# Bias rows as two one-pass products of stacked parts, and the gate's columns turned from a zeroed tile of 128

## The chip, the cores and the metric

The kernel runs on 1 core of one Trainium2 chip. The metric is the device time of one execution in microseconds (us). The kernel before takes 1168.48 us, the median of 3 runs (1168.42 to 1168.51).

## The reference

The kernel computes a two-layer encoder trunk for 512 tokens of width 1024, all in fp32. Layer 0 is differential attention with a shared relative-position bias; layer 1 is chunked gated linear attention (GLA). Both also attend to 256 memory tokens, and each is followed by a gated MLP with a short causal convolution. Two small pieces matter here.

```python
# layer 0: the bias that is added to the logits of each head
bias = table[t5_bucket(key_pos[None, :] - q_pos[:, None])]      # table = rel_bias, 32 x 6
logits = logits + jnp.transpose(bias, (2, 0, 1))[None, :, None]
# layer 1: the decay of each key channel, from 16 columns of the projection
log_a = jax.nn.log_sigmoid((gate_low @ gate_w + gate_b)) / GLA_GATE_TAU
```

## The kernel before, in words

**Work on TensorE.** Every large product is split: a tile is written as a high part in fp32r (a rounded fp32 that TensorE multiplies in one pass) and a low part, the remainder, and three fp32r products (high x high, high x low, low x high) add up in one PSUM bank. `split` and `split_weights` (L252 to L256, L309 to L311) make the parts: ScalarE (ACT) writes the high part, VectorE (DVE) subtracts to get the low part.

**Order.** TensorE runs in program order throughout. In the opening stage (L437 to L517, the tile pool "ini") ACT, DVE, POOL and SP run in program order too; elsewhere a scheduler orders these four. So in the opening stage an instruction that waits holds up everything written behind it on its engine.

**The opening stage.** It multiplies the normalised input with the first weight block in eight steps `k` = 0 to 7 of 12 matmuls each (L510 to L517), into four banks `first`. Ahead of step k the loop makes the operands of step k+1 (`operands`, L472 to L488). In step 4, ahead of its matmuls, `bias_rows` (L394 to L399) multiplies the bias table `rb` (32 x 6, fp32) with the one-hot matrix `oh` (32 x 640, fp32): two products on 32 rows and 6 columns of the array, each evicted by a DVE copy to 6 partitions of `bs`. In step 6 come, ahead of its matmuls: three weight blocks (`make_block`: ACT L253, DVE L256), the token sums of squares (`token_rsqrt`, L424, then L234 on DVE, L241 and L242 on ACT, and L227 to L229 on DVE), the fourth weight block, `small_vectors` (seven scalings of `cols`, then `lam`: a product and a sum on DVE, L404 and L405, an Exp on ACT, L406, and `nlam` on DVE, L407), and two writes of `bs` to DRAM (L506). Step 7 has only its matmuls. The projection of `v` (`gemm`, L330 to L332) follows at once on TensorE.

**Loads.** SP issues the loads in program order; as built, each one also waits for the one eight places ahead of it in that queue to land. Behind the loads of x and of the first weights come the first columns of the constants, `rb`, `oh`, three weight blocks of 512 KB, `cols`, the lambda vectors, the rest of the constants, the convolution columns and the fourth weight block. `bias` (L699 to L703) later reads the bias rows back from DRAM, shifted for each partition, for the first logits (L726).

**The gate in layer 1.** The projection `gm` gives 16 gate columns and 256 memory-query columns for each of four token blocks; ACT evicts them (`ev_gl`, L851 to L853), the gate columns to `gl` (128 x 4 x 16). `turn_gate` (L893 to L899) transposes the four blocks on TensorE (L896, recorded at L220), each as a product on 16 columns of the array, and makes the parts: two ACT copies (L897, L898) and a DVE subtraction (L899). The decay products (L909) wait for these.

**Tiles.** `xtile()` hands out 512-column tiles of a shared pool of 36 (tag "xs"); a tile's first writer waits until the older tile in that place is released.

Of the kernel before, what the change touches and what calls it, by code (L numbers as in the profile page):

```python
# [11 lines left out]
F32 = mybir.dt.float32  # L12
F32R = mybir.dt.float32r
# [9 lines left out]
KT = D // 128  # L23
NB = S // 128
# [155 lines left out]
def trunk(ctx, tc, head_d, x_t, mem_t, wpack, cols_a_d, cols_d, conv_d, gate_d, rel_bias, diff_lambda, consts, onehot, out):  # L180
    nc = tc.nc
    mm = nc.tensor.matmul
    V, A, G = nc.vector, nc.scalar, nc.gpsimd
# [9 lines left out]
    def bank(tag):  # L193
        return ps.tile([128, 512], F32, name=f"ps_{tag}", tag=tag)

    def xtile():
        return xs.tile([128, S], F32, name="xt", tag="xs", bufs=XS)

    def split_tiles(pool=None, tag="xs", bufs=XS):
        pool = pool or xs  # L200
        return (pool.tile([128, S], F32R, name=tag + "h", tag=tag, bufs=bufs),
                pool.tile([128, S], F32R, name=tag + "l", tag=tag, bufs=bufs))
# [4 lines left out]
    def blk(b, w=128):  # L207
        return slice(w * b, w * b + w)
# [9 lines left out]
    def transpose(dst, src):  # L218
        n = src.shape[0]
        nc.tensor.transpose(dst, src, ident[:n, :n])  # L220
# [31 lines left out]
    def split_weights(c, raw, hi, lo, pin=False):  # L252
        ins = A.copy(hi[:, c], raw[:, c])  # L253
        if pin:
            tc.keep_in_program_order(ins)
        V.tensor_sub(lo[:, c], raw[:, c], hi[:, c].bitcast(F32))  # L256

    def raw_tile():
        return wp.tile([128, WTILE], F32, name="raw", tag="raw", bufs=3)

    def load_raw(raw, n):
        nc.sync.dma_start(raw[:, :n], wpack[at[0], :, :n])
        at[0] += 1
        return raw
# [30 lines left out]
    def weights(key, by_block=False):  # L295
        i = used[0]
        assert plan[i][0] == key, (plan[i][0], key)
        limit = first_of[i] + WB if by_block else first_of[min(i + 2, len(plan))]
        while done[0] < min(max(limit, first_of[i + 1]), len(order)):
            make_block()  # L300
        used[0] += 1
        parts, made[i] = made[i], None
        return parts
# [5 lines left out]
    def split(hi, lo, src, gain):  # L309
        A.activation(hi, src, AF.Copy, scale=gain)  # L310
        V.scalar_tensor_tensor(lo, src, gain, hi.bitcast(F32), op0=ALU.mult, op1=ALU.subtract)  # L311
# [47 lines left out]
    bias_d = dr.tile([6, 640], F32, name="bias_d")  # L359
# [9 lines left out]
    def col(i, t=cols):  # L369
        return t[:, i:i + 1]  # L370
# [20 lines left out]

    def bias_rows(rb, oh, bs):  # L394
        for c in (slice(0, 512), slice(512, 640)):
            n = c.stop - c.start
            p = bank("lg")
            mm(p[:6, :n], rb, oh[:, c], start=True, stop=True)
            V.tensor_copy(bs[c.start // 512], p[:6, :n])  # L399

    def lam(lv, lp):
# [12 lines left out]
    def squares(src, acc):  # L414
        sq = xtile()
        A.activation(sq, src, AF.Square)
        if acc[0] is not None:
            V.tensor_add(sq, sq, acc[0])
        acc[0] = sq

    def token_rsqrt(tag, sq, nb, y, on_dve=False):
        p = bank(tag)
        for b in range(nb):
            mm(p[:, b:b + 1], sq[:, blk(b)], ones[:, 0:1], start=True, stop=True)  # L424
        return rsqrt(p[:, :nb], nb, 1.0 / D, on_dve, y=y)
# [10 lines left out]
    load = nc.sync.dma_start  # L436
    with tc.tile_pool(name="ini", bufs=1) as ip, tc.manual_schedule(engines={E.Activation, E.DVE, E.Pool, E.SP}):  # L437
        idle = ip.tile([128, 512], F32, name="idle")
        rb = ip.tile([32, 6], F32, name="rb")
        oh = ip.tile([32, 640], F32, name="oh")  # L440
        bs = xtile()[:6], xtile()[:6, :128]
        lv = xtile()[:, :256]
        G.memset(idle, 0.0)
        p = bank("tp")
        for n in (512, 320):
            mm(p[:, :n], idle[:, 0:128], idle[:, :n], start=True, stop=True)


        raws = [ip.tile([128, WTILE], F32, name=f"raw{i}") for i in range(4)]
        for t in (blk(0, S // 2), blk(1, S // 2)):  # L450
            A.dma_start(raws[0][:, t], wpack[0, :, t])
        head = ip.tile([128, 32 + S], F32, name="head")
        for c in (slice(0, 32 + S // 2), slice(32 + S // 2, 32 + S)):
            load(head[:, c], head_d[:, c])
        xT[0] = head[:, 32:]
        for k in range(1, KT):
            xT[k] = xtile()
            load(xT[k], x_t[k])
            load(raws[k // 2][:, blk(k % 2, S)], wpack[k // 2, :, blk(k % 2, S)])
        load(cols_a, cols_a_d)  # L460
        at[0] = 4
        load(C[:, 384:512], consts[:, 384:512])
        load(rb, rel_bias)
        load(oh, onehot)
        second = [load_raw(raw_tile(), WTILE) for _ in range(3)]
        load(cols, cols_d)
        load(lv, diff_lambda[0].rearrange("a b -> (a b)").partition_broadcast(128))
        parts, acc, split_w = [], [None], [None]
        made.append(parts)
        done[0] = 4  # L470

        def operands(k):  # L472
            if k % 2 == 0:
                split_w[0] = [wp.tile([128, WTILE], F32R, name=n, tag=n, bufs=WB) for n in ("whi", "wlo")]
            c = blk(k % 2, S)
            hi, lo = split_w[0]
            xh[k], xl[k] = split_tiles()
            if k == 0:
                for t in (blk(0, S // 2), blk(1, S // 2)):
                    V.tensor_copy(hi[:, t], raws[0][:, t])  # L480
                V.tensor_sub(lo[:, c], raws[0][:, c], hi[:, c].bitcast(F32))
                for t in (blk(0, S // 2), blk(1, S // 2)):
                    split(xh[0][:, t], xl[0][:, t], xT[0][:, t], col(0, head))
            else:
                split(xh[k], xl[k], xT[k], col(k, head))
                split_weights(c, raws[k // 2], hi, lo)
            parts.append((hi[:, c], lo[:, c]))
            squares(xT[k], acc)  # L488

        operands(0)  # L490
        for k in range(KT):
            if k + 1 < KT:
                operands(k + 1)
            if k == 0:
                second.append(load_raw(raws[0], WTILE))
            if k == 4:
                bias_rows(rb, oh, bs)
            if k == KT - 2:
                for j in range(4):
                    if j == 3:  # L500
                        token_rsqrt("lg", acc[0], NB, r_x[:, 0])
                    make_block(second)
                weights(("qk", 0), True)
                small_vectors()
                for c in range(2):
                    load(bias_d[:, 512 * c:min(512 * c + 512, 640)], bs[c])  # L506
            hi, lo = parts[k]
            terms = (xh[k], hi), (xh[k], lo), (xl[k], hi)
            full, left, right = slice(0, S), blk(0, S // 2), blk(1, S // 2)
            todo = [(b, i, full) for b in range(NB) for i in range(3)]  # L510
            if k == 0:
                todo = [(0, 0, left), (1, 0, left), (0, 0, right), (1, 0, right)] + sorted(
                    [u for u in todo if u[:2] not in ((0, 0), (1, 0))], key=lambda u: u[1])
            for b, i, t in todo:
                xp, w = terms[i]
                mm(first[b][:, t], xp[:, blk(b)], w[:, t], start=k == 0 and i == 0 and t is not right,
                   stop=k == KT - 1 and i == 2)  # L517

    load(C[:, 0:384], consts[:, 0:384])
    for i in range(4):  # L520
        load(memT[i], mem_t[i])
# [309 lines left out]
    def gla_layer(pool, mix, acc):  # L831
# [3 lines left out]
        k = pool.tile([128, NB, 384], F32, name="k", bufs=1)  # L835
        v = pool.tile([128, NB, 768], F32, name="gv", bufs=1)
        rr = pool.tile([128, NB, 768], F32, name="rr", bufs=1)
        gl = pool.tile([128, NB, 16], F32, name="gl", bufs=1)
        gl3, gw3 = split_tiles()
        gl3, gw3 = gl3[:96], gw3[:96, :384]  # L840
        rq, rh = small("rq", 2), small("rh", 1)
# [6 lines left out]
        def copy(dst, src, b, sc=r):  # L848
            A.activation(dst, src, AF.Copy, scale=sc[:, b:b + 1])

        def ev_gl(b, p):  # L851
            copy(gl[:, b], p[:, :16], b)
            copy(qm[:, b], p[:, 16:], b)  # L853

        def ev_r(b, p, off, w):
# [37 lines left out]
        def turn_gate(i):  # L893
            p = bank("tp")
            for b in range(NB):
                transpose(p[:16, blk(b)], gl[:, b])  # L896
            A.copy(gl3[0:16], p[:16])  # L897
            A.copy(gl3[64:80], p[:16])  # L898
            V.tensor_sub(gl3[32:48], p[:16], gl3[0:16].bitcast(F32))  # L899
# [361 lines left out]
```

## Time and profile before

| | |
|---|---|
| median of 3 runs | 1168.48 us |
| the profiled execution's own time | 1168.01 us |
| its span, first to last instruction | 1166.2 us |
| granted TensorE clock | 1.000 |
| busy TensorE (PE), weight loads (PEld), DVE, ACT, POOL | 1160.7, 965.3, 750.9, 545.5, 5.0 us |
| DMA | 117.68 MB, mean 101 GB/s |

The profile gives starts and durations of one execution, counted from its first instruction. PE lines are matmuls, PEld lines their weight loads, SPq lines the issue of a DMA by SP. In a timeline row the columns are start, duration, engine, line of the kernel, operation, output<-inputs, for a matmul the part of the array (rows*columns), its shape, and how many; a bracket at the end gives how long the engine had been idle and what released it. Matmuls overlap, so what one costs is the distance between starts, not its duration.

### The profile page before, as it was taken

The page shows a single profiled execution, that of the slowest core. Times are in us where ns is not written, and L with a number is a line of the kernel's source. Part 1 is how long each engine was busy: PE and PEld are TensorE (multiplying, and loading weights), DVE is VectorE, ACT ScalarE, POOL GpSimd, SP SyncE. Part 2 cuts the span into 40 slices and gives each one's busy share as a digit, 9 for nine tenths or more (in the row PEclk, how much of TensorE's full clock was granted, in tenths as well). Part 3 has the DMA queues.
Part 4 walks back from the last instruction along what each step waited for, and adds up shares of the span by engine and source line. Part 5 has one row for each costly group of instructions (what it writes and reads, how often), then busy time and mean ns, then how long its engine had stood idle before and what let it go on. Part 6 is the DMA issues. An engine that isn't in the chain of part 4 may idle for free.

```text
span 1166.2 us, 14790 instructions
## 1 busy us (share of the span) xinstructions
PE 1160.7 (100%) x5658; PEld 965.3 (83%) x5658; DVE 750.9 (64%) x1256; ACT 545.5 (47%) x951; POOL 5.0 (0%) x27
## 2 busy tenths in 40 slices
PE   9999999999999999999999999999999999999998
PEld 7888888888888888888888888988888888888887
DVE  7576778688677326677447637777876743576741
ACT  6676687555344213344437634436643421343420
POOL 0000000000000000000000000000000000000000
PEclk9999999999999999999999999999999999999999
DMA  8423242123223223222342230333232323232231
GB/s 295 158 70 99 78 141 73 63 103 130 85 90 120 83 88 124 75 91 98 120 148 68 81 108 3 110 121 109 93 123 73 98 102 108 85 114 73 89 101 45
DMA packets 39556, 117.68 MB, mean 101 GB/s; under 512 B 4703, under 2 KB 7192, under 8 KB 39486
## 3 DMA queue, kind: packets, MB, share of 16 engines
q1 hardware_dynamic: 39054, 116.35, 29.5%
q8 instruction: 44, 0.72, 0.3%
q10 hardware_dynamic: 432, 0.39, 0.1%
q14 instruction: 26, 0.21, 0.1%
HBM read 112.52 MB, written 4.21 MB: 100 GB/s over the span
## 4 chain that ended last, share of the span: by engine, by line
PE 98%; ACT 1%; DVE 1%; issue 0%; POOL 0%; DVEq 0%; POOLq 0%
PE ps_mm L352 9%; PE ps_mm L351 9%; PE ps_mm L353 9%; PE ps_sm L353 8%; PE ps_sm L352 8%; PE ps_sm L351 7%; PE ps_mm L330 6%; PE ps_mm L332 6%; PE ps_mm L331 6%; PE ps_tp L353 3%; PE ps_lg L353 3%; PE ps_lg L352 3%; PE ps_tp L352 3%; PE ps_lg L351 3%; PE ps_tp L351 3%; PE ps_tp L220 3%
## 5 line engine op out<-in xcount | busy, mean ns | idle before, releaser
L253 ACT CAST whi<-raw 128x1024 fp32r<-128x1024 f32 (+4 forms) x212 | 207.6, 986 | 245.4 <-PE ps_tp L352 120.9
L256 DVE TENSOR_TENSOR wlo<-raw,whi 128x1024 fp32r<-128x1024 f32 (+4 forms) x212 | 240.3, 1140 | 117.5 <-ACT whi L253 116.6
L351 PE MATMUL ps_mm<-xsh,whi 128*128 128x512 f32 x438 | 171.6, 392 | 0.0
L352 PE MATMUL ps_mm<-xsl,whi 128*128 128x512 f32 x438 | 170.6, 389 | 0.0
L353 PE MATMUL ps_mm<-xsh,wlo 128*128 128x512 f32 x438 | 170.5, 389 | 0.0
L351 PE MATMUL ps_sm<-xsh,whi 128*128 128x512 f32 x378 | 147.0, 389 | 0.0
L352 PE MATMUL ps_sm<-xsl,whi 128*128 128x512 f32 x378 | 147.0, 389 | 0.0
L353 PE MATMUL ps_sm<-xsh,wlo 128*128 128x512 f32 x378 | 147.0, 389 | 0.0
L330 PE MATMUL ps_mm<-whi,xsh 128*128 128x512 f32 (+2 forms) x336 | 129.1, 384 | 0.0
L332 PE MATMUL ps_mm<-whi,xsl 128*128 128x512 f32 (+2 forms) x336 | 126.1, 375 | 0.0
L331 PE MATMUL ps_mm<-wlo,xsh 128*128 128x512 f32 (+2 forms) x336 | 125.9, 375 | 0.0
L1113 ACT ACTIVATE cvo<-u,cv 128x512 f32<-128x512 f32 x88 | 71.4, 815 | 112.1 <-DVE u L1111 112.1
L352 PEld LDWEIGHTS ps_mm<-xsl,whi 128*128 128x128 f32 x438 | 82.3, 188 | 17.2 <-DVE xsl L311 0.4
L351 PEld LDWEIGHTS ps_mm<-xsh,whi 128*128 128x128 f32 x438 | 82.2, 188 | 17.1 <-issue 0.3
L353 PEld LDWEIGHTS ps_mm<-xsh,wlo 128*128 128x128 f32 x438 | 82.2, 188 | 17.1
L1114 DVE SCALAR_TENSOR_TENSOR cvo<-u,cv,cvo 128x512 f32<-128x512 f32 x88 | 65.7, 749 | 36.2 <-ACT cvo L1113 36.0
L352 PEld LDWEIGHTS ps_sm<-xsl,whi 128*128 128x128 f32 x378 | 70.9, 188 | 14.8
L351 PEld LDWEIGHTS ps_sm<-xsh,whi 128*128 128x128 f32 x378 | 70.9, 188 | 14.7
L353 PEld LDWEIGHTS ps_sm<-xsh,wlo 128*128 128x128 f32 x378 | 70.9, 188 | 14.7
L332 PEld LDWEIGHTS ps_mm<-whi,xsl 128*128 128x128 f32 x336 | 63.2, 188 | 11.6
L330 PEld LDWEIGHTS ps_mm<-whi,xsh 128*128 128x128 f32 x336 | 63.2, 188 | 11.3 <-ACT ks L659 0.3
L331 PEld LDWEIGHTS ps_mm<-wlo,xsh 128*128 128x128 f32 x336 | 63.3, 188 | 10.4
(295 smaller groups left out, 1760.1 us busy)
## 6 DMA issues: line engine op xcount, KB each, us to landing
raw<-in_wpack_dram SPq DMA_DIRECT2D x178, 512.0 KB, 3.5
xt<-in_x_t_dram SPq DMA_DIRECT2D x15, 256.0 KB, 5.2
raw<-in_wpack_dram SPq DMA_DIRECT2D x15, 256.0 KB, 3.0
raw<-in_wpack_dram SPq DMA_DIRECT2D x8, 384.0 KB, 3.0
xres<-xt SPq DMA_DIRECT2D x8, 256.0 KB, 3.0
xt<-xres SPq DMA_DIRECT2D x8, 256.0 KB, 5.4
out_dram<-xt SPq DMA_DIRECT2D x7, 256.0 KB, 2.0
bt<-bias_d SPq DMA_DIRECT2D x6, 256.0 KB, 4.1
```

The source lines that it names most:

```text
L220: nc.tensor.transpose(dst, src, ident[:n, :n])
L253: ins = A.copy(hi[:, c], raw[:, c])
L256: V.tensor_sub(lo[:, c], raw[:, c], hi[:, c].bitcast(F32))
L330: mm(p, sh[k][:, blk(b)], hi, start=k == 0, stop=False)
L331: mm(p, sh[k][:, blk(b)], lo, start=False, stop=False)
L332: mm(p, sl[k][:, blk(b)], hi, start=False, stop=k == KT - 1)
L351: mm(p, hi[:, blk(n)], bh, start=i == first, stop=False)
L352: mm(p, hi[:, blk(n)], bl, start=False, stop=False)
L353: mm(p, lo[:, blk(n)], bh, start=False, stop=i == last)
L1113: A.activation(c, u[:, 2:], AF.Identity, scale=cv[l][:, 2, j:j + 1], bias=cv[l][:, 3, j:j + 1])
L1114: V.scalar_tensor_tensor(c, u[:, 1:S + 1], cv[l][:, 1, j:j + 1], c, op0=ALU.mult, op1=ALU.add)
```

## The change

`bias_rows` gets a weight tile `rs` of 128 x 128 in fp32r, zero but for two blocks in its first six columns: rows 0 to 31 hold the table's high part, rows 32 to 63 the remainder. The one-hot matrix is loaded twice, stacked, copied to fp32r by POOL, with zero rows 64 to 127. One fp32r product over the whole array then adds both parts. The call moves from step 4 to step 7, ahead of its matmuls and behind all that step 6 puts on DVE; the two writes to DRAM move behind the opening stage. In layer 1 the gate columns go to a zeroed 128-column tile, and each transpose takes all 128 columns.

```diff
-    def bias_rows(rb, oh, bs):
+    def bias_rows(rb, rs, oh, bs):
+        V.tensor_copy(rs[:64, :6], rb)
+        V.tensor_sub(rs[32:64, :6], rb[32:64], rs[32:64, :6].bitcast(F32))
         for c in (slice(0, 512), slice(512, 640)):
             n = c.stop - c.start
             p = bank("lg")
-            mm(p[:6, :n], rb, oh[:, c], start=True, stop=True)
+            mm(p[:, :n], rs, oh[:, c], start=True, stop=True)
             V.tensor_copy(bs[c.start // 512], p[:6, :n])
...
-        rb = ip.tile([32, 6], F32, name="rb")
-        oh = ip.tile([32, 640], F32, name="oh")
+        rb = ip.tile([64, 6], F32, name="rb")
+        rs = ip.tile([128, 128], F32R, name="rs")
+        oh_raw = ip.tile([64, 640], F32, name="oh_raw")
+        oh = ip.tile([128, 640], F32R, name="oh")
...
         G.memset(idle, 0.0)
+        G.memset(rs.bitcast(F32), 0.0)
+        G.memset(oh[64:128].bitcast(F32), 0.0)
...
-        load(rb, rel_bias)
-        load(oh, onehot)
+        for i in range(2):
+            load(rb[32 * i:32 * i + 32], rel_bias)
+            load(oh_raw[32 * i:32 * i + 32], onehot)
+        G.tensor_copy(oh[:64], oh_raw)
...
-            if k == 4:
-                bias_rows(rb, oh, bs)
+            if k == KT - 1:
+                bias_rows(rb, rs, oh, bs)
             if k == KT - 2:
...
                 small_vectors()
-                for c in range(2):
-                    load(bias_d[:, 512 * c:min(512 * c + 512, 640)], bs[c])
...
+    for c in range(2):
+        load(bias_d[:, 512 * c:min(512 * c + 512, 640)], bs[c])
     load(C[:, 0:384], consts[:, 0:384])
...
-        gl = pool.tile([128, NB, 16], F32, name="gl", bufs=1)
+        gl = xtile().rearrange("p (b n) -> p b n", b=NB)
+        G.memset(gl, 0.0)
...
-            copy(gl[:, b], p[:, :16], b)
+            copy(gl[:, b, :16], p[:, :16], b)
...
-                transpose(p[:16, blk(b)], gl[:, b])
+                transpose(p[:, blk(b)], gl[:, b])
```

## The prediction

> **What bounds the kernel now.** I read the page first (busy shares and the chain that ended last), then PE's waits, then the timeline of each engine around the two places that the change touches.
>
> ```profile
> PE 1160.7 (100%) x5658; PEld 965.3 (83%) x5658; DVE 750.9 (64%) x1256; ACT 545.5 (47%) x951; POOL 5.0 (0%) x27
> PE 98%; ACT 1%; DVE 1%; issue 0%; POOL 0%; DVEq 0%; POOLq 0%
> PE ps_tp L446 <- POOL idle L443: 1.3, 1, 1.3
> PE ps_lg L909 <- DVE xsh L899: 0.4, 1, 0.4
> ```
>
> PE is 98% of the chain, and behind the start its longest wait is 0.4 us (the last two rows are the two longest: total, times, longest). So time put into or taken out of PE's sequence, a new wait of PE included, reaches the end nearly one for one; work on other engines costs only where PE comes to wait for it.
>
> **The change, part by part.**
>
> *1. The old bias products go.* PE's timeline:
>
> ```profile
> 15.68 0.39 PE L516 MATMUL ps_sm<-whi,xsl 128*128 128x512 f32 x1
> 16.00 1.24 PE L398 MATMUL ps_lg<-oh,rb 32*6 32x512 f32 x4
> 17.17 0.50 PE L516 MATMUL ps_mm<-whi,xsh 128*128 128x512 f32 x1
> 17.51 0.40 PE L516 MATMUL ps_mm<-wlo,xsh 128*128 128x512 f32 x1
> 26.23 0.39 PE L516 MATMUL ps_sm<-whi,xsl 128*128 128x512 f32 x1
> 26.46 0.39 PE L516 MATMUL ps_mm<-whi,xsh 128*128 128x512 f32 x1
> ```
>
> An undisturbed product of 512 columns takes 0.23 us from start to start (26.23 to 26.46). The two fp32 products, recorded as four matmuls, stretch 15.68 to 17.17: 1.49 - 0.23 = 1.26. The first matmul behind them takes 0.34 instead of 0.23: 0.11 more. Together 1.37 us go. Step 7, which starts at 26.46, could then start at 25.09.
>
> *2. The new products wait for DVE.* They stand ahead of step 7 and read `rs`, which DVE writes behind the whole of `small_vectors`. The decisive question is when DVE gets there. DVE's timeline:
>
> ```profile
> 15.17 0.69 DVE L418 TENSOR_TENSOR xt<-xt 128x512 f32<-128x512 f32 x1
> 17.06 0.88 DVE L399 COPY xt<-ps_lg 6x512 f32<-6x512 f32 x2 [1.21 <-PE ps_lg L398]
> 17.86 0.73 DVE L311 SCALAR_TENSOR_TENSOR xsl<-xt,head,xsh 128x512 fp32r<-128x512 f32 x1
> 21.59 3.48 DVE L256 TENSOR_TENSOR wlo<-raw,whi 128x1024 fp32r<-128x1024 f32 x3
> 25.91 0.16 DVE L228 SCALAR_TENSOR_TENSOR rs_t<-rs_t,rs_v 128x4 f32<-128x4 f32 x1
> 26.10 0.16 DVE L229 SCALAR_TENSOR_TENSOR r_x<-rs_t,r_x 128x4 f32<-128x4 f32 x1
> 26.65 1.23 DVE L256 TENSOR_TENSOR wlo<-raw,whi 128x1024 fp32r<-128x1024 f32 x1 [0.38 <-ACT whi L253]
> 29.37 0.16 DVE L407 SCALAR_TENSOR_TENSOR nlam<-l 128x1 f32<-128x1 f32 x1 [0.55 <-ACT l L406]
> 31.71 1.87 DVE L387 TENSOR_REDUCE ss<-xt 128x8 f32<-128x512 f32 x3 [2.18 <-ACT xt L386]
> ```
>
> The old bias copies also delayed DVE. Without the wait of 1.21 and the two copies, L311 follows L418 about 0.60 us after its start, the usual distance there: at 15.77 instead of 17.86, **2.09 us earlier**. Does all behind it keep that lead? ACT's timeline gives the inputs, in which the loads show as well:
>
> ```profile
> 19.83 1.05 ACT L253 CAST whi<-raw 128x1024 fp32r<-128x1024 f32 x1 [0.26 <-DVE xt L418]
> 25.18 0.26 ACT L241 ACTIVATE r_x<-ps_lg,eps 128x4 f32<-128x4 f32 x1 [4.29 <-DVE rs_v L234]
> 25.58 1.03 ACT L253 CAST whi<-raw 128x1024 fp32r<-128x1024 f32 x1
> 29.12 0.22 ACT L406 ACTIVATE l<-l 128x2 f32<-128x2 f32 x1
> ```
>
> DVE's third block subtraction moves from about 23.9 (two thirds into the 3.48) to 21.8; its high part is there at 20.88, so it holds the lead. The square root (L241) waits for DVE on ACT, and so does all behind it there; the fourth block's subtraction starts at 26.65 - 2.09 = 24.56. L405 ended 0.55 before `nlam`, at 28.82, and now ends at 26.73. Exp (L406), which queued behind evictions until 29.12, stands ahead of them in the new build: about 26.77 to 26.99. `nlam` follows at 27.03 (0.04 for each hand-over, an estimate). The copy to `rs` needs no result of `nlam`: 0.08 behind it, an estimate between nothing and its 0.16. The subtraction comes 0.20 later (the distance of the dependent pair 25.91, 26.10), lasts 0.16, and ends at 27.47. PE can start at **27.53**; it has been free since 25.09. It stalls **2.44 us**.
>
> *3. The new products themselves.* Nearest rows, the first fp32r product behind a wait (in the gate) and transposes of 128 columns:
>
> ```profile
> 48.22 0.60 PE L220 MATMUL ps_tp<-C,qs 128*128 128x128 f32 x4
> 48.66 0.60 PE L220 MATMUL ps_tp<-C,ks 128*128 128x128 f32 x4
> 623.74 0.47 PE L909 MATMUL ps_lg<-xsh,xsl 96*96 96x512 f32 x1 [0.38 <-DVE xsh L899]
> 624.05 0.39 PE L909 MATMUL ps_sm<-xsh,xsl 96*96 96x512 f32 x1
> ```
>
> The product of 512 columns costs 0.31 behind a wait (623.74 to 624.05). No row has an fp32r product of 128 columns: it lies between 0.06 (a quarter of 0.23) and 0.23. I take 0.11, the nearest by size: four transposes of 128 columns take 0.44 (48.22 to 48.66). Step 7 starts at 27.53 + 0.31 + 0.11 = 27.95 instead of 26.46: **+1.49 us**.
>
> *4. What moves beside it.* Loads: a second table and a second one-hot matrix (32 x 646 x 4 bytes, 83 KB) go ahead of the weight blocks. SP's issues, and the window 16 to 17 us (its last number is GB/s):
>
> ```profile
> 12.28 1.63 SPq L262 DMA_DIRECT2D raw<-in_wpack_dram  x3
> 16.00:17.00 1.00, 1.00 (x5) 0.26 (x4) 0.00 (x0) 1.00 (x3) 0.00 (x0) 1.00 0.91 344
> 19.79 0.28 SPq L506 DMA_DIRECT2D bias_d<-xt  x1
> ```
>
> The last of these rows waits, as built, for the third block, so that block landed at about 19.77. Its delay lies between 0.24 (83 KB at 344 GB/s) and 1.3 (two issue steps of about 0.65, as three issues fill 1.63). That ends its high part at 21.1 to 22.2, against 21.8 on DVE: 0 to 0.4 us. I take 0, and keep 0.4. POOL's copy of `oh` has no row; its loads are issued ahead of the blocks, so they have landed by 19.8, and the copy has 5 us before 25.09. The bias copies (0.88) move behind the new products on DVE, to about 28 to 29; behind them stands L387, with 2.18 us idle in front at 31.71. The DRAM writes now wait for these copies on SP, with three memory loads, the reads of the bias and the next weight blocks (38.17 before) queued behind them. The first use of the bias is at 54.97:
>
> ```profile
> 38.17 17.24 SPq L262 DMA_DIRECT2D raw<-in_wpack_dram  x6
> 54.97 0.55 DVE L726 CUSTOM_DVE_ANT_0 xt<-ps_lg,bt 128x384 f32<-128x384 f32 x1
> ```
>
> Both leave several microseconds, so I cost them at nothing; without that cover the 0.88 of the copies would be the price, or the part of the way to 54.97 by which the bias came late.
>
> *5. The gate.* The timeline of all engines, the tile view of `gl`, and POOL's timeline:
>
> ```profile
> 619.90 1.19 ACT L386 ACTIVATE xt<-qm 128x512 f32<-128x512 f32 x2
> 620.03 0.60 PE L220 MATMUL ps_tp<-C,gl 128*16 128x128 f32 x4
> 620.38 0.48 PE L330 MATMUL ps_mm<-whi,xsh 128*128 128x512 f32 x1
> 620.94 0.56 ACT L897 CAST xsh<-ps_tp 16x512 fp32r<-16x512 f32 x1
> L220 PEld LDWEIGHTS ps_tp<-C,gl x4: 88/88/90, 619.8 to 620.2; 128*16 128x16 f32 x4
> 585.70 0.42 POOL L888 MEMSET xt<- 96x384 f32 x1 [4.22 <-DVE xt L418]
> 592.81 0.52 POOL L903 MEMSET xt<- 96x512 f32 x1 [6.11 <-DVE xt L418]
> ```
>
> Four transposes on 16 columns take 0.35 (620.03 to 620.38), four on 128 columns 0.44: at most +0.09. But PE later waits 0.38, at 623.74, for a chain that starts with ACT's copy at 620.94, and ACT is busy with L386 until then, so the 0.09 is swallowed: **0**, and 0.09 if ACT were free. POOL zeroes tiles of this stage some 30 us ahead of the transposes, one of them more. One more shared tile shifts the pool's places by one; the built order on PE is the same, and I take 0.
>
> The Trainium skill ("TensorE: Matmul & The Clock Gate", section LDWEIGHTS) speaks against the wider tiles: a load lasts its columns divided by 1.2 per ns, so 107 ns for 128 columns against 13 for 16. By it four loads would cost 0.37 us more, estimated from that page, if nothing hid them; the row of 88 ns for 16 columns doesn't agree.
>
> *Sum:* -1.37 (old products) + 2.44 (stall) + 0.42 (new products) = **+1.49 us**, with the bounds +1.4 to +2.0 (128 columns at 0.06 to 0.23, load delay 0 to 0.4). The profiled execution's own 1168.01 (span 1166.2 and 1.8 around it) lies 0.47 below the median; the same shift on the median 1168.48 gives **1170.0** (1169.9 to 1170.5).
>
> **The rivals.**
>
> *A. On time.* If DVE had `rs` ready by 25.09, the wait would be nothing and the change would give -1.37 + 0.23 + 0.11 = -1.03: 1167.5. For it: PE would have its products at a third of the price. Against it: of DVE's chain only the 0.38 and 0.55 at 26.65 and 29.37 are waits, both for ACT, and its lead would have to be 4.5 us rather than 2.09 (27.53 + 2.09 - 25.09). A special case is that the change does not do what it says, and the products go in several passes as before: then the wait stays, and 1170.0 becomes 1171 (three more passes of about 0.3 us). Chance of A 0.10, of the special case 0.03.
>
> *B. The clock after the stall.* The first matmuls of the program ran at half speed:
>
> ```profile
> 1.31 3.14 PE L446 MATMUL ps_tp<-idle 128*128 128x512 f32 x4 [1.31 <-POOL idle L443]
> ```
>
> Two passes of 512 + 320 columns, 1664 in 3.14 us, are 1.9 ns per column; the old bias products, two passes of 640, took 1.17 us from 16.00 to 17.17, 0.9 ns. (The page shows a full granted clock there; the matmuls' own rows tell otherwise.) If the new stall is long enough to bring that state back, some 3.1 us of work behind it runs at half speed, +1.6: 1171.6, slower by 0.26%. It decides at the length of stall from which PE cools; the longest wait behind the start is 0.38, so no row here excludes 2.44. Chance 0.13. The Trainium skill (the same page, Part 1) asks for an idle window of about 3.4 us before the clock halves; by that 2.44 would not do it, and B would fall; no run here shows it.
>
> *C. The loads or the shifted tiles.* If the blocks come later than two issue steps, or a shifted tile place holds PE up, the price grows past +2.0; places came free 7 us apart on POOL (L888 at 585.70, L903 at 592.81), so it could be anything up to that: 1170.5 to 1175.5. Against it: as built, PE waits for no further engine outside the two places. Chance 0.07, half of it above 0.2%.
>
> **How the numbers follow.** Forecast 0.67: 1170.0. A measurement of this kernel can tell about 0.2%, 2.3 us, from no change; the forecast of +0.13% lies within. The range 1168.5 to 1171.7 holds the forecast's bounds, the special case and B, and leaves out A and most of C (0.10 + 0.07); it reaches 1.4 below the lowest sum because the stall is a difference of two long chains, and half of it could be off. Faster by over 0.2% would need more than the old products cost (1.37): 0.02, out of the forecast's own error. Slower: B 0.13 and half of C, 0.16. Same: the rest, 0.82.
>
> **What would show it.** In the changed profile: PE's waits name the new products with about 2.5 us, released by DVE's subtraction to `rs`; DVE's L311 of step 6 starts near 15.8; `nlam` runs near 27.0, ahead of the evictions; step 7 starts near 27.95. If the products start without a wait, part 2 is wrong, and A holds. If the matmuls of step 7 behind the stall lie about 0.45 us apart instead of 0.23, B holds. If `rs` comes later than 27.9, look at the high part of the third or fourth block and the landing of its load. L909 should still wait, by some 0.3 us, in the gate; if PE's distance from the transposes to L909 grows by 0.1, part 5 is wrong.

## The result and the profile after

The kernel with the change takes **1173.81 us** (median of 6 runs, 1173.39 to 1176.67); the kernel before took 1168.49 us beside it (6 runs, 1168.31 to 1169.61). The ratio is 1.0047, with a 95% interval of 1.0035 to 1.006: slower by 5.3 us, where 1.5 were forecast and 1171.7 was the upper end of the range. The profiled execution took 1173.54 us with a span of 1171.5, so the span grew by 5.3 as well (1166.2 before).

PE's waits in the kernel after (total, times, longest). The first row is new:

```profile
PE ps_lg L400 <- DVE rs L396: 3.9, 1, 3.9
PE ps_tp L452 <- POOL idle L447: 1.3, 1, 1.3
PE ps_lg L985 <- DVE xt L979: 0.2, 1, 0.2
```

So the place is the forecast one, the products' wait for `rs`, but it lasts 3.9 us. Behind the start no other wait passes 0.2 us: the late bias copies and DRAM writes, and the gate, hold PE up nowhere. PE's timeline around the wait (start, duration, then as before):

```profile
13.81 0.39 PE L522 MATMUL ps_mm<-whi,xsh 128*128 128x512 f32 x1
...
25.42 0.39 PE L522 MATMUL ps_sm<-whi,xsl 128*128 128x512 f32 x1
29.73 0.53 PE L400 MATMUL ps_lg<-oh,rs 128*128 128x512 f32 x2 [3.92 <-DVE rs L396]
30.09 0.45 PE L522 MATMUL ps_mm<-whi,xsh 128*128 128x512 f32 x1
...
30.62 0.63 PE L522 MATMUL ps_mm<-whi,xsl 128*128 128x512 f32 x1
31.05 0.63 PE L522 MATMUL ps_mm<-whi,xsh 128*128 128x512 f32 x1
...
34.26 0.39 PE L522 MATMUL ps_sm<-whi,xsl 128*128 128x512 f32 x1
34.49 0.39 PE L330 MATMUL ps_mm<-whi,xsh 128*128 128x512 f32 x1
```

The start of step 3, which lies ahead of all that the change moves on PE, and the start of the projection, in the kernel before:

```profile
13.19 0.39 PE L516 MATMUL ps_mm<-whi,xsh 128*128 128x512 f32 x1
...
29.18 0.39 PE L330 MATMUL ps_mm<-whi,xsh 128*128 128x512 f32 x1
```

Two terms can be read off. Step 7 starts at 30.09 instead of 26.46: **3.63 us**. And its twelve matmuls take 4.40 us (30.09 to 34.49) instead of the 2.72 of before (26.46 to 29.18, where the projection started): **1.68 us**. Together 5.31, the whole growth of the span between these two executions. A part of the 3.63 is not the change's: this execution's step 3 starts at 13.81, 0.62 later than before, and in run 2, whose opening stage is the same, at 13.01. Of the 5.3 by medians, on the other hand, some 0.25 lies outside the span (last section). The matmuls from 30.62 to 31.05 lie 0.43 apart, almost twice 0.23. The windows of this execution tell why (stretch, share of the core's span, busy share and count of PE, PEld, DVE, ACT and POOL, granted clock of PE, DMA share, GB/s):

```profile
29.00:30.00 1.00, 0.27 (x1) 0.30 (x2) 0.40 (x3) 0.12 (x1) 0.00 (x0) 1.00 0.21 80
30.00:31.00 1.00, 1.00 (x5) 0.82 (x4) 0.76 (x2) 0.00 (x0) 0.00 (x0) 0.79 0.05 16
31.00:32.00 1.00, 1.00 (x4) 0.76 (x3) 0.11 (x1) 0.58 (x2) 0.00 (x0) 0.50 0.04 12
...
33.00:34.00 1.00, 1.00 (x3) 0.75 (x3) 0.00 (x0) 0.56 (x3) 0.00 (x0) 0.50 0.73 231
34.00:35.00 1.00, 1.00 (x6) 0.81 (x5) 0.00 (x0) 1.00 (x3) 0.00 (x0) 1.00 0.90 330
```

The granted clock is 0.50 in the windows from 31 to 34, and 0.79 in the one before: a mean of 0.79 means 0.42 us of it at half speed, so half speed began at 30.58. It lasted until 34.0, some 3.4 us.

Why was `rs` so late? DVE's timeline of the same execution:

```profile
18.06 1.20 DVE L311 SCALAR_TENSOR_TENSOR xsl<-xt,head,xsh 128x512 fp32r<-128x512 f32 x1
...
20.40 3.87 DVE L256 TENSOR_TENSOR wlo<-raw,whi 128x1024 fp32r<-128x1024 f32 x3
24.18 0.15 DVE L234 TENSOR_SCALAR rs_v<-ps_lg 128x4 f32<-128x4 f32 x1
...
26.71 1.22 DVE L256 TENSOR_TENSOR wlo<-raw,whi 128x1024 fp32r<-128x1024 f32 x1 [1.26 <-ACT whi L253]
...
29.15 0.16 DVE L409 SCALAR_TENSOR_TENSOR nlam<-l 128x1 f32<-128x1 f32 x1 [0.27 <-ACT l L408]
...
29.43 0.15 DVE L396 TENSOR_TENSOR rs<-rb,rs 32x6 fp32r<-32x6 f32 x1
```

Three things differ from the forecast chain: the last step's L311 lasts 1.20 us (0.73 before, the row below), the three block subtractions take 3.87 (3.48), and the fourth waits 1.26 (0.38) for ACT's high part.

```profile
19.73 0.73 DVE L311 SCALAR_TENSOR_TENSOR xsl<-xt,head,xsh 128x512 fp32r<-128x512 f32 x1
```

ACT's and SP's timelines give the reason for the last two. ACT, SP, POOL, and last SP in the kernel before:

```profile
20.62 1.05 ACT L253 CAST whi<-raw 128x1024 fp32r<-128x1024 f32 x1 [1.72 <-DMA raw<-in_wpack_dram]
...
25.64 1.04 ACT L253 CAST whi<-raw 128x1024 fp32r<-128x1024 f32 x1 [0.76 <-DMA raw<-in_wpack_dram]
```

```profile
12.18 0.31 SPq L471 DMA_DIRECT2D oh_raw<-in_onehot_dram  x1
...
14.23 2.12 SPq L262 DMA_DIRECT2D raw<-in_wpack_dram  x3
...
19.34 5.28 SPq L262 DMA_DIRECT2D raw<-in_wpack_dram  x4
```

```profile
16.90 1.82 POOL L472 CAST oh<-oh_raw 64x640 fp32r<-64x640 f32 x1 [14.81 <-DMA oh_raw<-in_onehot_dram]
```

```profile
11.64 0.32 SPq L464 DMA_DIRECT2D oh<-in_onehot_dram  x1
...
17.37 0.36 SPq L262 DMA_DIRECT2D raw<-in_wpack_dram  x1
```

ACT now waits for the weight blocks to land. SP issued them at 14.23 instead of 12.28, because two more loads stand in front (2.05 us from the first one-hot load at 12.18 to the blocks, 0.64 before), and the rest, 0.54, is that SP came to the first one-hot load later in this execution (12.18 against 11.64). The fourth block went out at 19.34 instead of 17.37.

### The profile page after: what moved, and what is told of

Same layout as the page of the kernel before. It is cut to its first block, busy times and chain, and to the rows that moved or that the text cites. A ratio compares the mean times of both kernels' runs of the same rounds, so it can differ in the third digit from the quotient of the medians.

```text
span 1171.5 us, 14796 instructions
## 1 busy us (share of the span) xinstructions
PE 1162.1 (99%) x5656; PEld 967.4 (83%) x5656; DVE 751.3 (64%) x1258; ACT 546.2 (47%) x951; POOL 8.1 (1%) x31
## 4 chain that ended last, share of the span: by engine, by line
PE 96%; DMA 2%; DVE 1%; SPq 0%; ACT 0%; issue 0%; DVEq 0%
PE ps_mm L351 9%; PE ps_mm L353 9%; PE ps_mm L352 9%; PE ps_sm L353 7%; PE ps_sm L351 7%; PE ps_sm L352 7%; PE ps_mm L330 6%; PE ps_mm L332 6%; PE ps_mm L331 6%; PE ps_tp L353 3%; PE ps_lg L353 3%; PE ps_tp L352 3%; PE ps_lg L352 3%; PE ps_lg L351 3%; PE ps_tp L351 3%; PE ps_tp L220 3%
## 5 line engine op out<-in xcount | busy, mean ns | idle before, releaser
L256 DVE TENSOR_TENSOR wlo<-raw,whi 128x1024 fp32r<-128x1024 f32 (+4 forms) x212 | 240.4, 1139 | 120.3 <-ACT whi L253 119.2
L330 PE MATMUL ps_mm<-whi,xsh 128*128 128x512 f32 (+2 forms) x336 | 129.2, 384 | 0.0
L330 PEld LDWEIGHTS ps_mm<-whi,xsh 128*128 128x128 f32 x336 | 63.2, 188 | 11.3 <-ACT ks L667 0.3
```

The lines of the kernel that those rows point to most:

```text
L330: mm(p, sh[k][:, blk(b)], hi, start=k == 0, stop=False)
```

## The experiments

My theory: the loss is the forecast stall, grown by the late blocks and POOL's cast, plus half speed of PE behind a stall of this length. The rivals: the gate's wider tiles, the place of the products by itself, or a stall that has another cause than the order on DVE. "Before" in each ratio is the kernel before, measured beside it (medians 1168.36 to 1168.78 in the four sets).

**1. The gate alone**, put into the kernel before.

```diff
-        gl = pool.tile([128, NB, 16], F32, name="gl", bufs=1)
+        gl = xtile().rearrange("p (b n) -> p b n", b=NB)
+        G.memset(gl, 0.0)
...
-                transpose(p[:16, blk(b)], gl[:, b])
+                transpose(p[:, blk(b)], gl[:, b])
```

> The kernel before with only the gate's part of the change (zeroed tile of 128 columns, transposes on 128 columns). Theory W (all of the +5.3 us comes from the opening stage: TensorE waits for rs behind small_vectors on DVE, then runs at half speed): within 0.3 us of before, 1168.2 to 1168.8, no new wait in the gate. Rival G (the gate's wider transposes or the shifted places of the shared tiles cost part of it): at least 1 us above before, with longer waits or distances between TensorE's rows around 620 us.

Measured: 1168.11 us (11 runs), ratio 0.9998 [0.999, 1.0007]. PE's timeline at the transposes, and PE's wait behind them:

```profile
620.40 0.60 PE L220 MATMUL ps_tp<-C,xt 128*128 128x128 f32 x4
620.75 0.48 PE L330 MATMUL ps_mm<-whi,xsh 128*128 128x512 f32 x1
```

```profile
PE ps_lg L910 <- DVE xsh L900: 0.2, 1, 0.2
```

The four transposes take 0.35 us on 128 columns, as they did on 16 (620.03 to 620.38 before), so they cost PE nothing. From them to the first decay product, at 623.98, it takes 3.58 us (3.71 before). The wait behind them, 0.38 before, scatters with either gate: with the old one it is 0.34 in run 12 and below what the list shows in run 2. The gate is cleared.

**2. The bias alone**, the kernel after with the old gate: the diff of run 1 undone.

```diff
-                transpose(p[:, blk(b)], gl[:, b])
+                transpose(p[:16, blk(b)], gl[:, b])
```

> The changed kernel without the gate's part. Theory W: as slow as the changed kernel, 1173.4 to 1174.2. Rival G: faster than the changed kernel by what the gate costs, at least 1 us.

Measured: 1173.54 us (4 runs), ratio 1.004 [1.0026, 1.0054]. PE's wait for `rs` is 4.0 us and ends at 29.03. The granted clock is 0.50 from 29 to 31 us, 0.52 from 31 to 32, and falls ahead of the wait's end:

```profile
28.00:29.00 1.00, 0.00 (x0) 0.00 (x0) 0.58 (x4) 0.20 (x1) 0.00 (x0) 0.78 0.46 176
```

The loss is the bias change's, but for some 0.3 us outside the span (last section).

**3. The old products in the new place**: the kernel before with its two fp32 products ahead of step 7 and the DRAM writes behind the opening stage.

```diff
-            if k == 4:
+            if k == KT - 1:
                 bias_rows(rb, oh, bs)
...
-                for c in range(2):
-                    load(bias_d[:, 512 * c:min(512 * c + 512, 640)], bs[c])
+    for c in range(2):
+        load(bias_d[:, 512 * c:min(512 * c + 512, 640)], bs[c])
```

> The kernel before with only the move: the two old fp32 products on 32 rows go ahead of step 7, the DRAM writes behind the opening stage; no parts, no extra loads, no zero rows, gate as before. Theory W: the place alone costs nothing, since these products wait for no DVE work: 1168.2 to 1168.8. Rival (the place costs, by bias copies and writes that come later or by Exp ahead of the evictions): 1169.3 or more.

Measured: 1168.45 us (11 runs), ratio 0.9997 [0.9988, 1.0005], no new wait of PE. Moving the products costs nothing; they must only not depend on DVE. This kernel has no second loads and no cast on POOL, and so its DVE timeline tests the forecast of DVE's chain by itself:

```profile
17.58 0.74 DVE L311 SCALAR_TENSOR_TENSOR xsl<-xt,head,xsh 128x512 fp32r<-128x512 f32 x1
...
22.92 0.16 DVE L234 TENSOR_SCALAR rs_v<-ps_lg 128x4 f32<-128x4 f32 x1
...
27.11 0.16 DVE L407 SCALAR_TENSOR_TENSOR nlam<-l 128x1 f32<-128x1 f32 x1 [0.27 <-ACT l L406]
```

The forecast had the sum of squares' result `rs_v` at 22.91 (25.00 - 2.09) and `nlam` at 27.03. The arithmetic of that chain was right; what it left out is what this kernel lacks.

**4. The parts of `rs` early**: made at the start of step 6, ahead of its blocks, instead of inside `bias_rows`.

```diff
     def bias_rows(rb, rs, oh, bs):
-        V.tensor_copy(rs[:64, :6], rb)
-        V.tensor_sub(rs[32:64, :6], rb[32:64], rs[32:64, :6].bitcast(F32))
...
             if k == KT - 2:
+                V.tensor_copy(rs[:64, :6], rb)
+                V.tensor_sub(rs[32:64, :6], rb[32:64], rs[32:64, :6].bitcast(F32))
                 for j in range(4):
```

> The changed kernel, but DVE makes the two parts of the bias table ahead of the three weight blocks of step 6 and not behind small_vectors; the products stay ahead of step 7. Theory W: the products start without a wait, TensorE keeps full speed, and the time is before - 1.37 + 0.34, 1167.2 to 1167.8. Rival P (the products over the whole array, the extra loads or POOL's work are what costs): stays above 1169 although the wait for rs is gone.

Measured: 1169.49 us (11 runs), ratio 1.0013 [1.0004, 1.0022]: 4.3 us better than the kernel after, but not the forecast gain. The products start without a wait; a new one stands at the end of step 7. Its row in PE's waits, and ACT's timeline:

```profile
PE ps_mm L330 <- ACT ks L667: 1.9, 1, 1.9
```

```profile
29.11 0.20 ACT L406 ACTIVATE l<-l 128x2 f32<-128x2 f32 x1 [2.24 <-DVE l L405]
29.35 0.47 ACT L666 ACTIVATE qs<-ps_mm,r_x 128x256 f32<-128x256 f32 x1
```

The next projection needs a bank that ACT must first evict, and the evictions stand behind lam's Exp. In the kernel before they stood ahead of it (Exp at 29.12, first eviction at 28.04). Exp hangs on DVE's `lam`, behind the fourth block, which landed late. The stall moved from the products to the evictions. In the profile the clock stays at 1.00, but two of the 11 executions (1171.44 and 1173.51 us) have a mean granted clock of 0.998, so that half speed can follow in this kernel too; no trace shows their waits.

**5. The parts between**: behind the fourth block, but ahead of `small_vectors`.

```diff
                     make_block(second)
+                V.tensor_copy(rs[:64, :6], rb)
+                V.tensor_sub(rs[32:64, :6], rb[32:64], rs[32:64, :6].bitcast(F32))
                 weights(("qk", 0), True)
                 small_vectors()
```

> The changed kernel, but the parts are made behind the fourth weight block and ahead of small_vectors, so that TensorE's wait is shortened and not removed. From the changed profile: the block's subtraction ends at 27.9, the parts at 28.3, the stall is 2.6 us instead of 4.1. If the half speed follows a stall of this length too: 1168.5 + 2.2 + 1.7 = 1172.4. If it needs a stall of about 3.4 us or more: 1170.7, and the rows behind the products lie 0.23 us apart from the start.

Measured: 1171.91 us (5 runs), ratio 1.0036 [1.0023, 1.0048]. PE's wait and two windows of it:

```profile
PE ps_lg L398 <- DVE rs L510: 2.8, 1, 2.8
```

```profile
28.00:29.00 1.00, 1.00 (x4) 0.80 (x5) 0.81 (x8) 0.12 (x1) 0.00 (x0) 0.56 0.90 338
29.00:30.00 1.00, 1.00 (x4) 0.81 (x3) 0.88 (x3) 0.08 (x1) 0.00 (x0) 0.50 0.03 12
```

A wait of 2.8 us can thus be followed by half speed. Four of the five executions have a mean granted clock of 0.997 to 0.999; the fifth has 1.000 and still took 1171.82.

**6. One load each**: the table and the one-hot matrix stand doubled in DRAM, so that one DMA each fetches them.

```diff
-        for i in range(2):
-            load(rb[32 * i:32 * i + 32], rel_bias)
-            load(oh_raw[32 * i:32 * i + 32], onehot)
+        load(rb, rel_bias)
+        load(oh_raw, onehot)
```

> The changed kernel, but the table and the one-hot matrix lie stacked in DRAM already, and each is loaded by one DMA: the same bytes, two places fewer in SP's queue ahead of the weight blocks. Theory L (the two extra places delay the blocks by up to 1.3 us, and the fourth block's high part, 0.76 us late on ScalarE, carries that to rs): TensorE's wait for rs falls from 3.9 to about 2.6 us, 1172.5 if the half speed still follows, 1170.8 if not. Rival (the 83 KB or chance delay the blocks): the wait stays at 3.6 to 4 us, 1173.3 or more.

Measured: 1172.6 us (6 runs), ratio 1.0032 [1.002, 1.0044]. The three blocks are issued at 12.67, again 0.67 behind the one-hot load, the three subtractions take 3.48, and PE's wait falls from 3.9 to 3.2, still with half speed behind it:

```profile
PE ps_lg L400 <- DVE rs L396: 3.2, 1, 3.2
```

The two extra places in SP's queue thus cost 0.7 us of stall (1.3 was expected: the fourth block still waits 0.74 for its high part, 0.38 before the change); the times differ by 1.2 us, with intervals that overlap. One execution of this kernel kept the full clock and took 1170.44; the other five, with a mean granted clock of 0.997 to 0.999, took 1172.0 to 1174.0, which puts half speed at about 2 us by this one execution.

**7. One load each and the parts early** (4 and 6 together).

> e3_parts_early with the stacked loads. In e3 the wait moved to the first product of the next stage, 1.9 us for the evictions, which stand on ScalarE behind lam's Exp, which hangs on the fourth block. Theory L: this wait falls to 0.3 to 0.8 us and the time to 1167.9 to 1168.4. Rival (the blocks come as late as in e3): 1169.3 or more.

Measured: 1168.13 us (11 runs), ratio 0.9998 [0.9989, 1.0007]. The two repairs give back the whole loss, and the wait at the evictions shrinks with the earlier block; PE's timeline:

```profile
29.12 0.50 PE L330 MATMUL ps_mm<-whi,xsh 128*128 128x512 f32 x1 [0.41 <-ACT ks L666]
```

**8. `small_vectors` ahead of the fourth block**, with the parts early and the doubled loads as in the change.

```diff
                     if j == 3:
                         token_rsqrt("lg", acc[0], NB, r_x[:, 0])
+                        small_vectors()
                     make_block(second)
                 weights(("qk", 0), True)
-                small_vectors()
```

> e3_parts_early, but small_vectors (with lam's Exp on ScalarE) goes ahead of the fourth weight block and not behind it; loads as in the changed kernel. Theory E (the evictions wait because Exp, ahead of them on ScalarE, waits for DVE work that stands behind the fourth block): the wait of 1.9 us shrinks to the 0.6 us that the fourth block itself still costs, 1168.1 to 1168.5. Rival (the evictions wait for the fourth block itself, whose raw tile they overwrite): 1169.3 or more, the wait stays at 1.5 us or more.

Measured: 1169.08 us (11 runs), ratio 1.0006 [0.9998, 1.0015]. The wait fell from 1.9 to 0.4, as expected, but the time missed. I first read the rest as the late fourth block; run 9 showed that it was the order, and this kernel's ACT rows agree: the block's cast starts at 26.24, right behind Exp (26.13), with no wait for a landing.

**9. Runs 7 and 8 together.**

> Both loads stacked, the parts of the table's rows made early, and small_vectors ahead of the fourth block, so that the evictions L665 and L666 stand behind no Exp that hangs on that block. Theory (the wait at L330 came from the Exp behind the fourth block): no wait over 0.2 us at L330, and the old products' time is gained: 1168.4 - 1.37 + 0.4 = 1167.4 us, range 1167.2 to 1167.8. Rival (the evictions wait for the fourth block's own ScalarE work): a wait of 0.3 to 0.6 us stays at L330, and the time is that of the version with stacked loads and early parts, 1168.1 us.

Measured: 1169.2 us (11 runs), ratio 1.0003 [0.9994, 1.0011]. **The theory fell**: the wait at L330 grew to 1.2 us. DVE's, ACT's and PE's timelines:

```profile
27.57 1.23 DVE L256 TENSOR_TENSOR wlo<-raw,whi 128x1024 fp32r<-128x1024 f32 x1 [0.78 <-ACT whi L253]
```

```profile
28.95 0.48 ACT L665 ACTIVATE qs<-ps_mm,r_x 128x256 f32<-128x256 f32 x1 [1.42 <-PE ps_sm L521]
```

```profile
29.85 0.50 PE L330 MATMUL ps_mm<-whi,xsh 128*128 128x512 f32 x1 [1.17 <-ACT ks L666]
```

The first eviction is put down to PE, but its own bank had been full since about 26.6 (its last matmul starts at 26.21 and lasts 0.40). What ends just ahead of it is DVE's subtraction of the fourth block: 27.57 + 1.23 = 28.80, and the eviction starts 0.15 later. The same distance stands in the kernel before (27.88 and 28.04), in run 8 (28.53 and 28.69) and in run 10 (27.91 and 28.07). So the rival is right in kind, the fourth block, but by DVE's subtraction and not by ACT's work, and larger than it said: the first eviction waits for this subtraction, and whoever puts `small_vectors` ahead of it delays the evictions. Why it waits was not tried. By the kernel, the fourth block is read from `raws[0]`, a tile of the pool "ini", and `qs` and `ks`, which the evictions write, come from a pool opened behind it; that they lie in its place is likely, and not shown.

**10. The cast of the one-hot matrix on ACT**, between the third block and the token sums; else as run 9.

```diff
-        G.tensor_copy(oh[:64], oh_raw)
...
                     if j == 3:
+                        A.copy(oh[:64], oh_raw)
                         token_rsqrt("lg", acc[0], NB, r_x[:, 0])
```

> As the version with all repairs, with the one-hot's cast on ScalarE instead of GpSimd. Theory (GpSimd's cast, beside it in time, makes VectorE's L311 of the last step last 1.20 us instead of 0.74): L311 back at 0.74 us, with the time that of the version with all repairs within 0.3 us, as VectorE has room there by then. Rival (L311 is longer because of a load or of its place): L311 stays at 1.20 us.

Measured: 1168.85 us (11 runs), ratio 0.9998 [0.9989, 1.0007], 0.35 less than run 9 beside it, with intervals that overlap; 0.3 or less was expected. DVE's timeline answers the question:

```profile
17.59 0.74 DVE L311 SCALAR_TENSOR_TENSOR xsl<-xt,head,xsh 128x512 fp32r<-128x512 f32 x1
```

L311 is back at 0.74, so the 0.46 came from POOL's cast.

**11. `lam` behind the opening stage**: run 7 with the cast on ACT and `lam` issued behind the stage, where the scheduler puts Exp behind three evictions.

```diff
-        lam(lv, xtile()[:, 0:128].rearrange("p (a b) -> p a b", a=2))
...
+    lam(lv, xtile()[:, 0:128].rearrange("p (a b) -> p a b", a=2))
     load(C[:, 0:384], consts[:, 0:384])
```

> Stacked loads, the parts early, the one-hot's cast on ScalarE, and lam's product, sum, Exp and nlam issued behind the opening stage, so that the scheduler puts the Exp behind three evictions, as before the change. The fourth block stands ahead of the scalings again. Theory (the first eviction waits for whichever is last of the Exp ahead of it, the fourth block's subtraction on VectorE, and its own bank): the subtraction ends near 26.2, the first eviction starts within 0.3 us behind it, no wait over 0.2 us at L330, L330 starts 2.7 to 2.8 us behind step 7's first product, and the time is 1168.4 - 1.37 + 0.35 = 1167.4 us, ratio 0.9991. Rival (the old products' time is not gained, since some other wait takes its place): a wait of 0.4 us or more, 1168.0 us or above.

Measured: 1168.29 us (11 runs), ratio 0.9995 [0.9987, 1.0004]. The mechanism came as forecast, the time, 1167.4, did not. ACT's and PE's timelines:

```profile
26.21 0.47 ACT L665 ACTIVATE qs<-ps_mm,r_x 128x256 f32<-128x256 f32 x1 [1.43 <-DVE wlo L256]
...
27.80 0.20 ACT L406 ACTIVATE l<-l 128x2 f32<-128x2 f32 x1 [0.39 <-DVE l L405]
```

```profile
12.97 0.39 PE L520 MATMUL ps_mm<-whi,xsh 128*128 128x512 f32 x1
...
25.09 0.45 PE L520 MATMUL ps_mm<-whi,xsh 128*128 128x512 f32 x1
...
27.92 0.39 PE L330 MATMUL ps_mm<-whi,xsh 128*128 128x512 f32 x1
```

Here the profile itself names the fourth block's subtraction as the releaser of the first eviction. Step 7 runs into the projection without a wait, 2.83 us from start to start. Since executions start differently, the gain is read from the start of step 3: from there to the projection it takes 14.95 us (12.97 to 27.92), 15.99 before (13.19 to 29.18). The 1.04 gained is what rival A gave to "on time" (1.03).

**12. The same with the old gate.**

> As the version with the Exp behind the opening stage, with the gate as it was before the change. Theory: the same time within the interval (1167.4 us), since the gate's change alone gave no difference; it is also a second measurement of the repaired bias. Rival (the gate's wider transposes cost 0.1 us or more in this build): 0.1 to 0.4 us less than that version.

Measured: 1167.59 us (11 runs), ratio 0.9992 [0.9983, 1.0001], 0.7 below run 11, with intervals that overlap. PE's timeline:

```profile
13.83 0.39 PE L520 MATMUL ps_mm<-whi,xsh 128*128 128x512 f32 x1
...
28.79 0.39 PE L330 MATMUL ps_mm<-whi,xsh 128*128 128x512 f32 x1
```

The opening takes 14.96 us from step 3, 14.95 in run 11, and from the projection to the end of the span both take 1137.0, as does the kernel before. So PE's rows show no price of the gate and a gain of 1.03 to 1.04; run 11 has 0.4 us more outside the span (last section), which is most of what its time missed. By medians the two repaired kernels are 5.5 to 6.2 us better than the kernel after, and 0.3 to 1.0 better than the one before; against the latter neither interval excludes no difference, so the times alone do not settle a gain of this size.

## Why the prediction was wrong, point by point

Two terms failed that the sum put at nothing: what moves beside the products (part 4), which made the stall 1.64 longer, and the clock behind the stall (rival B), 1.68. The place of the stall and its releaser were right.

- **Part 1, the old products (1.37):** 1.43 measured. From the start of step 3 to where PE is free for step 7 it took 13.27 before (13.19 to 26.46), and takes 11.84 after (13.81 to 25.65).
- **Part 2, the stall:** right in place, kind and releaser, wrong in size: 2.44 forecast, 4.08 measured (29.73 less the 25.65 at which PE was free). `rs` let the products start 2.20 later than forecast. `nlam` makes up 2.12 of this: 0.43 is the start of this execution (L311 of step 6 at 16.20, not 15.77; in run 2 it is at 15.81), which PE shares with its 0.56; 0.47 is L311 stretched by POOL; 0.39 is the second and third block; the remainder, 0.83, the fourth block.
- **Part 3, the new products (0.42):** 0.36 measured (29.73 to 30.09).
- **Part 4, what moves beside it: the step that failed.** The delay of the loads was bounded at 0 to 0.4 on the chain and taken as 0; it was about 1.2 (0.39 and 0.83). How it splits changes with the execution: in run 2 the three subtractions take 3.48, and the fourth alone is late, by a wait of 1.31. The queue step of two places was measured at 1.41 (2.05 less 0.64), close to the upper bound of 1.3 for the block's landing, but I followed it only to the third block and not to the fourth, whose issue moved by 1.97 (0.54 of it the later start of the loads) and whose landing ended ACT's wait at 25.64. Run 6 shows 0.7 of stall for the two places; the rest of the 1.2 was not taken apart. And POOL's cast was costed only by whether it is done in time, not by what DVE does beside it: 0.47. The sign named for a late `rs`, the landing of the third or fourth block, was the right one. The bias copies and the DRAM writes cost nothing, as forecast.
- **Part 5, the gate (0):** right, by run 1, but not for the reason given. There was no 0.09 for a wait to swallow: the transposes take 0.35 on 128 columns as on 16.
- **Rival B, the clock after the stall:** it happened. Its price was right, 1.6 forecast and 1.68 measured, with some luck, as nothing tied the 3.14 us at the program's start to the length of a later stretch (3.4); its chance of 0.13 was far too low, because it was set against a stall of 2.44 with the upper bound for the loads left out of it, and because the longest wait of the profile before (0.38) could neither show nor exclude it. No run has a wait of 2.44, so whether B would have come with the forecast stall stays open. The forecast's error is the 1.64 of stall and 1.68 of half speed; less 0.06 for the cheaper products and with the 0.56 by which PE itself was free later, that is the 3.82 between +1.49 and the span's +5.31.
- **Rival C:** the loads did come later than two issue steps; as a rival it was in the right place, and 1173.81 lies inside its 1170.5 to 1175.5, with a chance of 0.07, though the loads brought only some 1.2 of it. A shifted tile place did not show.

## What to carry to other kernels

When an operand of the bounding engine moves behind other work on a helper engine, write its place in that engine's program order first, and then every input of the work ahead of it, down to the queue place of each load: late blocks put some 1.2 us on the chain here, and two places fewer in the queue took 0.7 us of stall away. A stall on TensorE of some 3 us is to be priced with the half speed behind it (1.4 to 1.7 us in the four profiles that have it), not by its own length. Two profiles of this kernel are best compared from a row ahead of the change, as step 3 starts anywhere from 12.97 to 14.05 in them. And taking a wait away shows the next one: here it passed from the products to the evictions behind the Exp, and then to the evictions behind the fourth block.

## What the runs showed of the hardware

- **Half speed around the end of a wait.** PE waits of 3.9 (after), 4.0 (run 2), 3.2 (run 6) and 2.8 us (run 5) each came with a granted clock of 0.50 for 3.4 us; the 1.9 of run 4 did not, in its profile. In the kernel after, half speed began 0.85 us behind the end of the wait (30.58 against 29.73); in run 5 the window from 28 to 29, at 0.56, puts its start at about 28.1, 0.2 behind the wait's end at 27.93; in run 2 the same window, at 0.78, puts it at about 28.56, 0.5 ahead of the wait's end. From the products' start to the projection the four take 4.53 to 4.76 us; at full speed it would be about 3.08 (0.36 and 2.72), so half speed cost 1.4 to 1.7. The Trainium skill ("TensorE: Matmul & The Clock Gate", Part 1) describes a free-running window of about 3.4 us and half speed after an idle one. The length of half speed here, 3.4 us, and its changing distance from the wait agree with such windows; that a wait of 2.8 us suffices does not agree with a window that has to be idle throughout. PE worked for about 0.85 of the 3.4 us ahead of 30.58 in the kernel after, and for about 0.64 of those ahead of 28.1 in run 5. Executions with a mean granted clock of 0.997, such as the 1176.67 of the kernel after and two of run 5, took some 2 to 3 us more than the others; 0.003 of 1172 us is about 7 us at half speed, an estimate, or two such stretches, but no trace shows where.
- **POOL against DVE.** L311 of the last step lasts 1.20 or 1.21 us in all eight kernels with POOL's cast, and 0.74 or 0.75 where ACT does it (runs 10 to 12) or there is none (run 3). The cast lasts between 1.6 and 2.5 us, but in all eight it ends 0.65 to 0.67 behind the start of that L311 (16.90 + 1.82 less 18.06 in the kernel after). The Trainium skill ("SBUF — State Buffer", section "SBUF: two separate sides") says that a GpSimd instruction that reads SBUF and a DVE instruction with two inputs from SBUF lock each other out of a shared port for a whole instruction; a cast that ends at one fixed point of DVE's work, and a single DVE instruction stretched by 0.46, agree with it. Why the instructions ahead of it, such as L256 at 16.86 in the kernel after (0.68), keep their length beside the cast, no run shows.
- **Time outside the span.** It is 1.8 us in the kernel before and in the versions with the gate alone (run 1), the bias alone (run 2), the moved products (run 3) and the old gate (run 12), but 2.0 to 2.2 in every one that has both changes. That is 0.2 to 0.4 us which no engine's row shows; its cause stays open.
